# Five buffers for gathered rows and one residual tile, with the rows queued anew, in a streaming encoder step

## The chip, the cores and the metric

The kernel runs on one core of a Trainium2 chip. The time is device microseconds (us) of one execution. The engines are PE (TensorE), DVE (VectorE), ACT (ScalarE), POOL (GpSimd) and SP (SyncE), which here only issues transfers; POOL issues the gathers.

## The reference

One layer of a streaming encoder for 1024 prompt tokens and 32 sample tokens of width 1024, in f32:

```python
z = x @ w_in + b_in                       # split into 12 sections of 1024 columns
y_a = (a_b * conv3(a_c * a_x)) @ w_out_a                      # mixer A
y_b = (gelu(b_g) * rg_lru(conv4(b_x))) @ w_out_b              # mixer B
y_c = (rmsnorm(hgrn2(c_q, c_f, c_i)) * silu(c_g)) @ w_out_c   # mixer C, 8 heads
m = sigmoid(g_a)*y_a + sigmoid(g_b)*y_b + sigmoid(g_c)*y_c
x = layer_norm(ALPHA*x + m @ w_o)                             # x1 in the kernel
# peer: 8 heads, product keys, the best 16 of 16384 experts for each head and token
h = gelu(x . u[expert]);  out = sum_k g_k * h_k * v[expert_k] # 128 experts a token
x = layer_norm(ALPHA*x + out)
```

## The kernel before

The tokens go in two halves of 512 (the second with the 32 sample tokens). The first half runs through mixers, `norm1` (L878) and `topk` first. Its four tiles of 128 tokens then take the expert rows one by one: `gather` (L1206) issues for each of 128 places an indirect transfer on POOL that brings one row of 1024 floats for each of 128 tokens (a buffer `row` from `big`, L869), 128 times from table u and 128 times from v. DVE takes the dot of a u row with x1 (L1222), or adds a v row, scaled, to x1 (L1230). The tile `x1g` holds x1 and collects the sum; at the end of a tile `ln` (L861 to L867) normalises it, with two `row` buffers for its gain and bias (L874), and SP stores it. That makes 4 x 256 = 1024 row instructions on DVE.

The second half's experts are done densely: the one-hot tiles `oa` and `ob` (L1072, L1075) spread the chosen weights over all 16384 experts through PE, and `dense` (L1106 on, blocks D0 to D15) multiplies by all of u and v. A part of the hidden layer is computed ahead, beside the spread, and read back in D0 to D4 (`ge<-hd`).

PE's matmuls are made of three products of a high and a low part (L336, L337, L341). A weight comes as `wraw` by SP; ACT makes its high part `wh` (L295) and DVE its low part `wl` (L299), or `wl` is fetched again from DRAM. In `dense`, DVE and ACT make `w`, `dh` and `dl` (L1126 to L1131) from the hidden layer.

The row instructions run beside the second half. `BESIDE` says how many of them belong to each of seven stretches of the program: the end of the first half's topk with mixer A (92), the heads of mixer C (125), the outputs of mixers C and B (145), out_b1, norm1 and topk1 (94), retrieval and spread with the hidden layer ahead (42), D0 to D4 (82), D5 to D15 (444). `pacing` (L1248) puts row k of r of a stretch behind the DVE instruction that stands where k/r of the stretch's PE instructions have been written; `paced` holds a row instruction behind that place in DVE's order. It is an earliest place: a scheduler that plans with transfer times sets the final order of each queue at build time, and it plans with the number of buffers.

```python
x1 = self.gp.tile([128, D], F32, name="x1g", tag="x1g", bufs=X1G)
nc.sync.dma_start(x1[:n], self.x1d[g0:g0 + n, :])
```

Of the kernel before, what the change touches and what calls it, by code (L numbers as in the profile page):

```python
# [10 lines left out]
F32 = mybir.dt.float32  # L11
# [10 lines left out]
D = 1024  # L22
# [32 lines left out]
MARK = lambda nc, n: None  # L55


BESIDE = 92, 125, 145, 94, 42, 82, 444
AHEAD = 40
LATE = 4  # L60
ORDER = (0, 0), (0, 1), (0, 2), (0, 3), (1, 2), (1, 3), (1, 0), (1, 1)
# [8 lines left out]
PL2 = True  # L70
F2 = 1
FA = 2
X1G = 2
HEAD = 4
TAIL = 4

# [25 lines left out]
class K:  # L102
# [764 lines left out]
        V.tensor_add(dst[:n], r[:n], bias[:n])  # L867

    def big(self):  # L869
        return self.gp.tile([128, D], F32, name="row", tag="row", bufs=4)  # L870

    def lnvec(self, nm, pool=None, bufs=None):
        t = pool.tile([128, D], F32, name=nm, bufs=bufs) if pool else self.big()
# [332 lines left out]
    def gather(self, ti, g0, n, ex, gw):  # L1206
# [9 lines left out]

        x1 = self.gp.tile([128, D], F32, name="x1g", tag="x1g", bufs=X1G)
        nc.sync.dma_start(x1[:n], self.x1d[g0:g0 + n, :])
# [29 lines left out]
def pacing(ins, cuts, rows):  # L1248


    E, out = mybir.EngineType, []
    for i0, i1, r in zip(cuts, cuts[1:], rows):
        at, n, j = [], 0, 0
        for i in ins[i0:i1]:
            n += i.engine == E.PE
            if i.engine == E.DVE:
                at.append((n, i))
        n = int(n * (EARLY if i1 == cuts[-1] else 1.0))
        for k in range(r):
            while j + 1 < len(at) and at[j][0] < n * k // r:  # L1260
                j += 1
            out.append(at[j][1])
    return out


def build(tc, io):
    with ExitStack() as ctx:
# [64 lines left out]
        k.cuts.append(len(ins))  # L1332
        k.pace, k.npaced = pacing(ins, k.cuts, BESIDE), 0
        for t in todo:
# [63 lines left out]
```

## Time and profile before

| | us |
|---|---|
| median of 3 runs | 4093.62 |
| lowest and highest | 4083.32, 4103.83 |
| the profiled execution's own time | 4081.6 |
| its span in the profile | 4079.8 |

The span goes from the first to the last instruction of the profiled execution. Times in the views count from its start. Busy time of an engine is the sum of its instructions' durations; a wait is idle time of an engine and is put down to what ended it.

### The profile page before, as it was taken

The numbers are of one execution on the slowest core, as the hardware profiler recorded it, in microseconds if no ns is written. First come the engines' busy times: TensorE is split into PE (matmuls) and PEld (weight loads), VectorE is DVE, ScalarE is ACT, GpSimd is POOL, SyncE is SP. The second block draws the span as 40 slices with busy tenths as digits, with TensorE's granted clock in tenths as the row PEclk, the third lists the DMA queues.
The fourth block names the chain that finished last, engine by engine and source line by source line (L and its number), as shares of the span: only waits on it lengthen the run. The fifth ranks groups of instructions, "written<-read, shape, count | busy, mean of one in ns | idle before, by whom it ended". The sixth has DMA issues, their size and how long they took to land.

```text
span 4079.8 us, 69919 instructions
## 1 busy us (share of the span) xinstructions
PE 3794.9 (93%) x26917; PEld 3544.5 (87%) x26917; DVE 3139.8 (77%) x6578; ACT 1495.5 (37%) x2368; POOL 1537.8 (38%) x1353
## 2 busy tenths in 40 slices
PE   9999999999899898999778998799999999999996
PEld 7888787788899887999668998689999999999996
DVE  6556435579988887775679999788788888778888
ACT  3333327433232213563233588722222222222222
POOL 0000000001345544343333688723355555455553
PEclk9999999999999998999889999899999999999998
DMA  5443455678999887999997897798899988889996
GB/s 190 145 145 132 150 192 178 221 242 300 355 325 318 305 286 249 350 333 342 363 347 276 281 284 231 221 340 313 289 323 324 325 315 315 307 308 315 315 327 231
DMA packets 377230, 1132.94 MB, mean 278 GB/s; under 512 B 34816, under 2 KB 109696, under 8 KB 374848
## 3 DMA queue, kind: packets, MB, share of 16 engines
q1 hardware_dynamic: 229440, 591.53, 41.2%
q0 software_dynamic: 147456, 536.94, 37.5%
q8 instruction: 212, 3.47, 0.3%
q14 instruction: 122, 1.00, 0.1%
HBM read 1000.48 MB, written 127.84 MB: 277 GB/s over the span
## 4 chain that ended last, share of the span: by engine, by line
issue 12%; DVE 12%; DMA 10%; PE 9%; POOL 8%; ACT 1%; POOLq 0%; DVEq 0%; SPq 0%; ACTq 0%
POOL row L1213 8%; DMA row<-in_v,ex 8%; DVE x1g L1230 3%; PE z L341 3%; PE z L337 2%; PE z L336 2%; DVE oa L1072 2%; DMA row<-in_u,ex 2%; DVE wl L299 1%; PE t L1076 1%; DVE e L963 1%; DVE e L962 0%; DVE e L965 0%; DVE e L964 0%; DVE e L961 0%
## 5 line engine op out<-in xcount | busy, mean ns | idle before, releaser
L336 PE MATMUL z<-h,wh 128*128 128x272 f32 (+5 forms) x4608 | 1319.0, 313 | 43.0 <-ACT wh L295 25.5
L337 PE MATMUL z<-l,wh 128*128 128x272 f32 (+5 forms) x4608 | 1307.9, 311 | 1.2 <-DVE l L372 1.2
L1213 POOL DMA_INDIRECT row<-in_u,ex x512 | 621.2, 1213 | 1497.8 <-DVE ex L1036 651.6
L295 ACT CAST wh<-wraw 128x1024 fp32r<-128x1024 f32 x568 | 596.1, 1050 | 1419.2 <-PE z L337 1102.9
L336 PEld LDWEIGHTS z<-h,wh 128*128 128x128 f32 x4608 | 879.7, 191 | 89.1 <-ACT wh L295 28.7
L1213 POOL DMA_INDIRECT row<-in_v,ex x512 | 680.3, 1329 | 663.0 <-DVE x1g L1230 450.6
L337 PEld LDWEIGHTS z<-l,wh 128*128 128x128 f32 x4608 | 880.9, 191 | 37.6 <-issue 2.9
L341 PE MATMUL z<-h,wl 128*128 128x272 f32 (+5 forms) x4608 | 741.8, 309 | 7.5 <-DMA wl<-wl 6.6
L1230 DVE SCALAR_TENSOR_TENSOR x1g<-row,hh,x1g 128x1024 f32<-128x1024 f32 x512 | 654.9, 1279 | 119.5 <-DMA row<-in_v,ex 115.7
L1222 DVE SCALAR_TENSOR_TENSOR row<-row,x1g 128x1024 f32<-128x1024 f32 x512 | 619.3, 1219 | 152.6 <-DMA row<-in_u,ex 151.8
L341 PEld LDWEIGHTS z<-h,wl 128*128 128x128 f32 x4608 | 648.1, 189 | 42.4 <-DMA wl<-wl 8.0
L299 DVE TENSOR_TENSOR wl<-wraw,wh 128x1024 fp32r<-128x1024 f32 x400 | 488.4, 1222 | 188.4 <-ACT wh L295 88.1
L337 PE MATMUL z<-dl,wh 128*128 128x272 f32 x2048 | 521.0, 294 | 21.5 <-DVE dl L1131 21.1
L336 PE MATMUL z<-dh,wh 128*128 128x272 f32 x2048 | 516.4, 294 | 9.6 <-ACT dh L1130 8.9
L337 PEld LDWEIGHTS z<-dl,wh 128*128 128x128 f32 x2048 | 388.3, 194 | 27.7 <-DVE dl L1131 27.7
L336 PEld LDWEIGHTS z<-dh,wh 128*128 128x128 f32 x2048 | 386.3, 193 | 12.8 <-ACT dh L1130 12.1
L341 PE MATMUL z<-dh,wl 128*128 128x272 f32 x2048 | 284.6, 292 | 23.5 <-DVE wl L299 23.5
L341 PEld LDWEIGHTS z<-dh,wl 128*128 128x128 f32 x2048 | 270.5, 192 | 25.3 <-DVE wl L299 25.3
L1075 POOL TENSOR_SCALAR ob<-iota,tr 128x128 f32<-128x128 f32 x272 | 215.2, 805 | 34.8 <-ACT tr L1050 23.8
L1130 ACT CAST dh<-w 128x544 fp32r<-128x544 f32 x128 | 82.5, 648 | 374.4 <-DVE w L1126 360.6
L1076 PE MATMUL t<-ob,oa 128*128 128x128 f32 x1088 | 169.0, 294 | 30.8 <-DVE oa L1072 11.2
L1076 PEld LDWEIGHTS t<-ob,oa 128*128 128x128 f32 x1088 | 148.9, 201 | 44.3 <-POOL ob L1075 17.2
(379 smaller groups left out, 4600.4 us busy)
## 6 DMA issues: line engine op xcount, KB each, us to landing
wl<-wl SPq DMA_DIRECT2D x304, 512.0 KB
wraw<-in_w_in SPq DMA_DIRECT2D x192, 512.0 KB
wraw<-in_vt SPq DMA_DIRECT2D x128, 512.0 KB
wraw<-in_ut SPq DMA_DIRECT2D x128, 512.0 KB
gd<-stg SPq DMA_DIRECT2D x34, 1024.0 KB
gt<-gd SPq DMA_DIRECT2D x16, 2176.0 KB
wraw<-in_wq SPq DMA_DIRECT2D x56, 512.0 KB
wraw<-in_w_o SPq DMA_DIRECT2D x24, 512.0 KB
```

Of the source, the lines that this page charges most:

```text
L295: nc.scalar.copy(wh, raw)
L299: nc.vector.tensor_sub(wl, raw, wh.bitcast(F32))
L336: mm(ps[:, :n], wh[:, k, :], xh[:, o:o + n], start=k == 0, stop=False)
L337: mm(ps[:, :n], wh[:, k, :], xl[:, o:o + n], start=False, stop=False)
L341: mm(ps[:, :n], wl[:, k, :], xh[:, o:o + n], start=False, stop=k == KT - 1)
L1072: V.tensor_scalar(oa, self.iota, tr[:, 0, t:t + 1], tr[:, 2, t:t + 1], op0=OP.is_equal, op1=OP.mult)
L1075: G.tensor_scalar(ob, self.iota, tr[:, 1, t:t + 1], None, op0=OP.is_equal)
L1076: nc.tensor.matmul(pw[:, s * 128:(s + 1) * 128], oa, ob, start=True, stop=True)
L1130: A.copy(hi, w)
L1213: nc.gpsimd.indirect_dma_start(out=u[:n], out_offset=None, in_=self.io[tab], in_offset=bass.IndirectOffsetOnAxis(ap=ex[:n, s:s + 1], axis=0))
L1222: V.scalar_tensor_tensor(u[:n], u[:n], 1.0, x1[:n], op0=OP.mult, op1=OP.mult, accum_out=hh[:n, s:s + 1])
L1230: V.scalar_tensor_tensor(x1[:n], u[:n], hh[:n, s:s + 1], x1[:n], op0=OP.mult, op1=OP.add)
```

## The change

`row` gets five buffers in place of four, `x1g` one in place of two (SBUF for one buffer of 128 x 1024 floats goes from one to the other). The number of row instructions rises from 145 to 185 beside the outputs and from 94 to 135 in out_b1, norm1 and topk1; it falls from 42 to 30 beside retrieval and spread, from 82 to 40 in D0 to D4 and from 444 to 417 in D5 to D15. The first two numbers stay, and so does the sum of 1024.

```diff
-BESIDE = 92, 125, 145, 94, 42, 82, 444
+BESIDE = 92, 125, 185, 135, 30, 40, 417
@@
-X1G = 2
+X1G = 1
@@
     def big(self):
-        return self.gp.tile([128, D], F32, name="row", tag="row", bufs=4)
+        return self.gp.tile([128, D], F32, name="row", tag="row", bufs=5)
```

## Rows read from the trace of the kernel before

**Rows 1.** The first two parts of the page: busy time of each engine with its share of the span, and the mean DMA rate in 40 equal slices of 102 us.

```profile
PE 3794.9 (93%) x26917; PEld 3544.5 (87%) x26917; DVE 3139.8 (77%) x6578; ACT 1495.5 (37%) x2368; POOL 1537.8 (38%) x1353
...
GB/s 190 145 145 132 150 192 178 221 242 300 355 325 318 305 286 249 350 333 342 363 347 276 281 284 231 221 340 313 289 323 324 325 315 315 307 308 315 315 327 231
```

**Rows 2.** The chain of work that ended last, shares of the span by engine and line.

```profile
POOL row L1213 8%; DMA row<-in_v,ex 8%; DVE x1g L1230 3%; PE z L341 3%; PE z L337 2%; PE z L336 2%; DVE oa L1072 2%; DMA row<-in_u,ex 2%; DVE wl L299 1%; PE t L1076 1%; DVE e L963 1%; DVE e L962 0%; DVE e L965 0%; DVE e L964 0%; DVE e L961 0%
```

**Rows 3.** Busy time of each engine in four stretches between row instructions at which `BESIDE` goes on (first and last row of a stretch, in DVE's order): the outputs' 145 rows, the 94 after them, the 82 of D0 to D4, the 444 of D5 to D15. Columns: stretch, its length, busy time (instructions), granted clock as a share of full, busy share of the DMA engines, GB/s.

```profile
1579.00:2026.00 447.00, 415.07 (x3075) 404.84 (x3074) 299.49 (x517) 203.18 (x295) 175.09 (x146) 0.96 0.92 342
2026.00:2366.00 340.00, 289.14 (x2162) 279.79 (x2163) 311.43 (x1036) 137.11 (x263) 158.90 (x147) 0.91 0.87 304
...
2650.00:2937.00 287.00, 268.09 (x1997) 262.00 (x1996) 228.58 (x357) 69.40 (x85) 87.54 (x82) 0.95 0.89 316
2937.00:4050.00 1113.00, 1076.39 (x8458) 1071.03 (x8456) 924.90 (x1180) 296.10 (x445) 600.44 (x441) 0.99 0.89 315
```

**Rows 4.** The instructions on the tile `row`: lowest, median and highest duration in ns, first and last start.

```profile
L1222 DVE SCALAR_TENSOR_TENSOR row<-row,x1g x512: 1196/1218/1292, 976.3 to 3730.8; 128x1024 f32<-128x1024 f32 x171
...
L1213 POOL DMA_INDIRECT row<-in_v,ex x512: 932/1178/5040, 1331.7 to 4043.0; - x171
L1230 DVE SCALAR_TENSOR_TENSOR x1g<-row,hh,x1g x512: 1175/1279/1400, 1341.3 to 4049.7; 128x1024 f32<-128x1024 f32 x171
```

**Rows 5.** The chain in order of time, in the stretch of D5 to D15: start, duration, what.

```profile
3119.00 8.20 DMA row<-in_v,ex
3131.02 5.38 DMA row<-in_v,ex
```

**Rows 6.** Waits from 2937 to 4050 us: who waited for what, us in total, times, longest.

```profile
POOL row L1213 <- DVE x1g L1230: 241.7, 180, 7.4
POOL row L1213 <- DVE row L1222: 202.7, 132, 7.4
DVE x1g L1230 <- DMA row<-in_v,ex: 84.6, 67, 5.6
...
DVE row L1222 <- DMA row<-in_u,ex: 64.3, 41, 7.1
```

**Rows 7.** Two lines of the program with their first and last start: the gates beside mixer B (their last one ends the outputs), and the products with the keys (the last one ends topk1 on PE).

```profile
L836 ACT ACTIVATE e<-z,hb x48: 480/496/693, 357.9 to 1838.8; 128x274 f32<-128x274 f32 x32, 128x512 f32<-128x512 f32 x16
...
L938 PE MATMUL t<-keys,e x288: 270/275/583, 880.1 to 2213.9; 128*128 128x128 f32 x128, 128*32 128x128 f32 x16
```

**Rows 8.** Busy time as in rows 3, in three other stretches.

```profile
1579.00:2110.00 531.00, 468.23 (x3427) 453.67 (x3427) 356.84 (x630) 225.07 (x348) 209.88 (x174) 0.94 0.93 344
2110.00:2600.00 490.00, 441.22 (x3349) 425.49 (x3349) 487.80 (x1631) 312.40 (x597) 318.82 (x341) 0.95 0.82 264
980.00:1060.00 80.00, 63.78 (x478) 60.47 (x477) 76.53 (x299) 25.65 (x39) 26.64 (x26) 0.96 1.02 398
```

**Rows 9.** The same view for instructions on the tile `row` alone; the columns are DVE (its dots count twice, with the read of their sum), POOL (one per gather), clock, DMA share and GB/s.

```profile
1579.00:2110.00 531.00, 215.40 (x303) 209.88 (x174) 0.94 0.93 344
2110.00:2600.00 490.00, 127.68 (x100) 125.22 (x100) 0.95 0.82 264
2600.00:2650.00 50.00, 10.24 (x8) 8.88 (x8) 0.93 0.77 241
```

**Rows 10.** DVE's waits for rows: from 976 to 1248 us (one line), from 1248 to 1579 us (two), from 1579 to 2110 us (two).

```profile
DVE row L1222 <- DMA row<-in_u,ex: 13.5, 11, 2.3
...
DVE x1g L1230 <- DMA row<-in_v,ex: 15.1, 11, 3.2
DVE row L1222 <- DMA row<-in_u,ex: 14.1, 12, 3.0
...
DVE row L1222 <- DMA row<-in_u,ex: 57.1, 42, 4.4
...
DVE x1g L1230 <- DMA row<-in_v,ex: 14.2, 10, 4.1
```

**Rows 11.** DVE's costliest groups from 2110 to 2600 us: busy us, mean ns, and the idle time before them with what ended it.

```profile
L1072 DVE TENSOR_SCALAR oa<-iota,tr 128x128 f32<-128x128 f32 x487 | 153.0, 388 | 0.2
L1230 DVE SCALAR_TENSOR_TENSOR x1g<-row,hh,x1g 128x1024 f32<-128x1024 f32 x100 | 127.7, 1277 | 1.9 <-DMA row<-in_v,ex 1.9
```

**Rows 12.** The end of a tile on DVE, from the instructions on the tile `x1g`.

```profile
L861 DVE BATCH_NORM_STATS2 lnst<-x1g x8: 665/676/694, 1691.2 to 4054.5; 128x6 f32<-128x512 f32 x8
...
L865 DVE TENSOR_SCALAR x1g<-x1g,lnmv x4: 794/808/812, 1696.6 to 4058.8; 128x1024 f32<-128x1024 f32 x4
L866 DVE TENSOR_TENSOR x1g<-x1g,row x4: 1215/1216/1224, 1697.5 to 4059.7; 128x1024 f32<-128x1024 f32 x4
```

**Rows 13.** Two transfers of 512 KB on the chain that ended last.

```profile
2069.02 12.73 DMA x1n<-in_x
...
4045.45 5.36 DMA row<-in_ln_b
```

**Rows 14.** PE on that chain: 16 matmuls of 128x272.

```profile
2671.09 2.00 PE z L341 x16
```

**Rows 15.** PE's waits from 2650 to 2937 us (one line) and from 2937 to 4050 us (three).

```profile
PE z L337 <- DVE dl L1131: 15.6, 12, 2.7
...
PE z L341 <- DVE wl L299: 23.5, 8, 5.6
PE z L336 <- ACT dh L1130: 6.1, 4, 2.8
PE z L337 <- DVE dl L1131: 5.5, 6, 2.0
```

## The prediction

> **What bounds the kernel now.** I read the busy totals first: PE is busy for 93% of the span, DVE for 77%, and POOL, which issues the gathers and builds one-hot tiles, for 38% [rows 1]. So PE is the engine to feed, and the question is what starves it. The chain that ended last does not run through PE alone: the gathers, as POOL's issue (8%) and as transfers (8% and 2%), hold some 18% of the span [rows 2]. The reader is to see there that the chain of gathered rows (buffer free, POOL issues, the row lands, DVE accumulates, buffer free) competes with PE for the end.
>
> Then the windows, cut where the list `BESIDE` hands over, that is at row 217, 362, 498 and 580 in the order of accumulation [rows 3]. Each row is 0.524 MB and its DVE instruction takes 1.22 us for u and 1.28 us for v [rows 4]. In the last stretch (D5 to D15) 444 rows in 1113 us are one each 2.51 us; with four buffers a buffer comes round each 10.0 us. That is what it needs: transfers on the chain there take 5.4 to 8.2 us, and issue (0.9 to 1.2 us) and accumulation are added [rows 4, 5]. POOL waits 445 us of this stretch for DVE to free a buffer, and DVE 149 us for rows to land [rows 6]: four buffers are just too few. DVE works in order, so behind a late row stands the split of the next weights (wl) and of the activations (dh, dl) for PE.
>
> The same holds earlier, by another sign. The last output gate beside mixer B is done at 1839 us [rows 7], but the 145 rows queued beside the outputs last until 2026 us, 190 us into the next stage [rows 3]. From 1579 to 2110 us there are 174 gathers, one each 3.05 us [rows 9]; the list asks for more than comes. So here it is not the list that sets the pace but the four buffers, and DVE still waits 71 us for rows in that stretch, 29 us in the heads, 13 us before [rows 10].
>
> Last, the stretch in which DVE is full: from 2110 to 2600 us (topk1, retrieval, spread) it is busy for 488 of 490 us [rows 8] and waits 1.9 us for rows; 100 rows take 128 us of it, beside 153 us of one-hot tiles [rows 11]. An added row there costs its full 1.28 us.
>
> **The change, part by part.**
>
> *Heads and before (976 to 1579 us), list unchanged.* The fifth buffer gives a row 25% more time. DVE's 42 us of row waits [rows 10] are the most that it can give back. The heads are a chain of short DVE and PE steps, so a DVE wait is often PE's too, but the weights are ahead of it; between all and nothing I take half: **-20** (0 to -42).
>
> *Outputs to norm1 (1579 to 2110 us), list 145 to 185 and part of 94 to 135.* If the buffers set the pace, five give 174 x 1.25 = 217 rows, 43 more. DVE has room: 357 busy of 531 us [rows 8], 55 more fit. DMA: 344 GB/s x 531 us = 183 MB, and 22.5 MB more make 205 MB, 386 GB/s. The 80 us from 980 us show 398 GB/s [rows 8], so it just fits; at the best of the 102 us slices, 363 GB/s [rows 1], it takes 565 us, +34. The 71 us of row waits can shrink, or stay if denser traffic makes rows later; half of them at most would be PE's. I take **-5** (-35 to +34), near the row of 398, because that one is as mixed with weights as this stretch.
>
> The Trainium skill, "DMA: Bandwidth & Descriptors", section "Where 436 GB/s comes from", says that a transfer between HBM and SBUF is bound by about 358 GB/s a core; by that figure the stretch would take 573 us, an estimate, and 42 us of gain would go. This trace does not agree over 80 us (398 GB/s [rows 8]) and nearly does over each 102 us slice (363 at most [rows 1]).
>
> *DVE-full stretch and the end of the spread (2110 to 2650 us).* Now it does 108 rows (100 and 8) [rows 9]. The new list has 92+125+185+135+30 = 567 rows up to the dense stage; with 217 + 217 = 434 done at 2110 us, 133 are left, 25 more: 25 x 1.28 = 32 us. The end of the second tile also moves here (row 512 is number 110 of the 135; before it was in D0 to D4): two statistics, one normalisation, two passes, 0.68 x 2 + 0.81 + 1.22 x 2 = 4.6 us [rows 12]. Sum **+37**. Bounds: if the fifth buffer speeds up nothing, 217 + 174 = 391 are done and 176 left, 68 more: +92. If rows kept to the list, which spreads 135 over the matmuls from 1839 us to the end of topk1 at 2214 us [rows 7], 98 of these and 217 + 185 = 402 before them were done and 67 left: -48. I take the middle, what five buffers give.
>
> *D0 to D4 (2650 to 2937 us), list 82 to 40.* PE does 1997 matmuls [rows 3]; at full rate 16 take 2.00 us [rows 14], so the floor is 250 us of the 287. What PE waits for there is dl, from DVE [rows 15]. 42 rows fewer take 54 us from DVE (229 busy) and 22 of 91 MB from DMA [rows 3]. I take two thirds of the 37: **-24** (-10 to -37).
>
> *D5 to D15 (2937 us on), list 444 to 417.* Floor 8458 x 0.125 = 1057 us of 1113. Rows come each 2.67 us; five buffers give each 13.3 us against the 10 it needs, so most of DVE's 149 us of row waits [rows 6] go, with 35 us of its work. PE's visible waits are 35 us, 24 of them for wl [rows 15], the rest of the 56 sits between. I take a little over half, **-30** (-10 to -50).
>
> *One residual tile instead of two.* Now the next tile's first dots run between the last passes of the one before. With one tile: last pass, store of y, load of x1, first dot. In SP's queue the weights stand behind that load, and in DVE's the splits for PE behind the first dot. A load of the same size took 12.7 us on the chain in heavy traffic, one at the end 5.4 us [rows 13]: a store and a load make 11 to 25 us a turn, three turns. DVE has other work in that time, and the next tile's rows are already being gathered; what it costs is what the queue order misjudges. Nothing in the trace shows that; I take **+8** (0 to +36, half of three long turns), nearer to nothing, since PE has weights in hand.
>
> Sum: -20 - 5 + 37 - 24 - 30 + 8 = **-34 us**. The profiled execution took 4081.6 us, 12 under the median of 4093.62; taken from the median, 4060 us.
>
> **Rivals.** About 0.5% (20 us) is what a measurement of this kernel can tell from no change: the three runs before lie within 20.5 us.
>
> *The chain of rows is the bound (larger gain).* 18% of the chain goes through rows [rows 2]. If so, the waits go nearly whole: -42 - 35 in front, -37 - 50 behind, against +37 + 8: about -119, 3975 us. For it: POOL's waits for buffers. Against: PE runs at 95% of full rate in D5 to D15 already.
>
> *DMA at its limit (no change).* If 363 GB/s is all that lasts, the outputs and norm1 cost +34 instead of -5: sum +5, 4099 us. For it: DMA moves 344 GB/s there at 0.93 of its engines. Against: the 398, at 1.02 [rows 8].
>
> *Rows pile up in the DVE-full stretch (slower).* The list asks for 567 rows before the dense stage whether or not they come in time, and what is late is done where DVE has no room. Break-even: the other terms make -20 - 5 - 24 - 30 + 8 = -71, so the stretch loses it all at +71, which is (71 - 5)/1.28 = 52 rows more, that is if only 407 are done at 2110 us: if the fifth buffer speeds the rows from 1579 us up by under 9%. With no speed-up (+92) and less to win behind (-10 - 15), the sum is -20 + 0 + 92 - 25 + 8 = +55, 4149 us. For it: rows here may be late because of DVE's queue and loaded DMA rather than the number of buffers. Against: in the last stretch four buffers' turn and a row's time are equal.
>
> **Chances.** Forecast (20 to 80 us gained) 0.48, larger gain 0.12, no change 0.22, slower 0.18. Faster 0.60, same 0.22, slower 0.18. The forecast's own range is 4014 to 4074. The range for 8 in 10 reaches halfway into the larger gain and into the slower case: 4005 to 4112 us.
>
> **What would show it.** DVE's waits for rows in D5 to D15 fall from 149 us to under 50; that stretch is some 30 us shorter, D0 to D4 24 us. From 1579 us to the end of norm1 the gathers come each 2.4 to 2.6 us at 380 GB/s or more. The spread ends later, measured from the end of norm1, by some 37 us. At the turns of a tile there are 11 to 25 us without a row. I am wrong if the rows between 1579 and 2110 us are no denser (then slower), if PE loses time there to late weights (DMA), or if the last stretch is no shorter although DVE no longer waits for rows: then PE was not waiting for DVE.

## The result, and the profile after

The change makes the kernel slower: 4119.42 us against 4087.81 us (medians of 7 runs each), a ratio of 1.0076 with a 95% interval of 1.0058 to 1.0095, some 32 us. The forecast was 34 us faster, the range ended at 4112. The profiled execution took 4113.9 us, with a span of 4112.1 us.

The page's busy line and its chain, for the changed kernel:

```profile
PE 3806.3 (93%) x26917; PEld 3552.8 (86%) x26917; DVE 3140.1 (76%) x6578; ACT 1507.7 (37%) x2367; POOL 1536.2 (37%) x1353
...
PE z L341 12%; PE z L336 12%; PE z L337 12%; PE t L1076 2%; DMA row<-in_u,ex 1%; DVE oa L1072 1%; DVE x1g L1230 1%; DVE row L1222 1%; DMA ge<-hd 1%; DMA row<-in_v,ex 1%; POOL row L1213 1%; DMA wl<-wl 1%; DVE e L963 0%; DVE e L962 0%; DVE e L965 0%
```

The rows have left the chain: 3% of the span, against 18% in [rows 2]. PE's matmuls hold it now. By this view alone the change did what it should; it is no view of the time.

The stretches between the places where the list goes on, as in [rows 3]: the 185 rows of the outputs, the 135 after them, the 40 of D0 to D4, the 417 of D5 to D15.

```profile
1569.00:2073.00 504.00, 454.91 (x3263) 435.10 (x3264) 360.76 (x602) 209.40 (x309) 226.00 (x187) 0.94 0.95 358
2073.00:2604.00 531.00, 446.39 (x3325) 433.12 (x3323) 504.86 (x1587) 289.37 (x551) 329.18 (x327) 0.90 0.86 287
...
2730.00:3012.00 282.00, 265.88 (x2017) 260.44 (x2017) 174.79 (x277) 67.44 (x85) 38.36 (x41) 0.97 0.70 241
3012.00:4060.00 1048.00, 1042.26 (x8295) 1041.28 (x8294) 883.76 (x1108) 302.65 (x442) 549.92 (x412) 1.00 0.90 321
```

The last row shows the gain: PE is busy for 1042 of 1048 us where it was for 1076 of 1113. DVE's waits from 3012 to 4060 us, to be set beside [rows 6], where rows made it wait 149 us:

```profile
DVE acc L1144 <- PE z L341: 75.5, 54, 4.8
DVE wl L299 <- ACT wh L295: 53.8, 43, 4.3
DVE row L1222 <- DMA row<-in_u,ex: 12.5, 8, 5.3
...
DVE x1g L1230 <- DMA row<-in_v,ex: 0.7, 3, 0.3
```

DVE now waits for PE, and 13 us for rows. Where the time went is seen when the traces are cut at events of the program instead of rows. The table is worked out from the traces: the ends are the last start of a line's instruction (attention L767 for the heads, L846 in out_b1, L906 for norm1, the keys' products L938 for topk1, the one-hot products L1076 for the spread), then the first `w` of D0, the first of D5 and the last matmul. Rows are the row instructions on DVE up to or in a stretch. The kernels from e1 on are those of the experiments. Each line is one traced execution, which lies up to 14 us from its kernel's median; e4_x1g's is the fastest of its ten.

| kernel | to heads' end | outputs, out_b1 | norm1 | topk1 | spread | to D0 | D0 to D4 | D5 to D15 | after PE | rows done by end of topk1 | rows in spread |
|---|---|---|---|---|---|---|---|---|---|---|---|
| before | 1571 | 380 | 140 | 123 | 417 | 23 | 287 | 1108 | 31 | 421 | 75 |
| after | 1561 | 398 | 143 | 129 | 489 | 18 | 285 | 1064 | 25 | 456 | 110 |
| e1_bufs | 1564 | 400 | 147 | 125 | 379 | 24 | 287 | 1064 | 30 | 452 | 45 |
| e2_list | 1575 | 385 | 142 | 121 | 440 | 30 | 312 | 1065 | 25 | 427 | 88 |
| e4_x1g | 1568 | 380 | 140 | 121 | 423 | 24 | 286 | 1105 | 32 | 418 | 78 |
| e7_more | 1563 | 395 | 147 | 129 | 497 | 27 | 295 | 1056 | 25 | 456 | 119 |
| e8_split | 1568 | 399 | 141 | 125 | 446 | 31 | 295 | 1065 | 25 | 452 | 88 |
| e5_late | 1563 | 396 | 147 | 115 | 362 | 18 | 300 | 1068 | 45 | 440 | 22 |
| e9_thin | 1568 | 382 | 101 | 114 | 431 | 28 | 336 | 1059 | 30 | 365 | 85 |
| e10_back | 1559 | 398 | 125 | 103 | 360 | 19 | 286 | 1086 | 125 | 405 | 22 |
| e11_none | 1560 | 399 | 140 | 126 | 379 | 24 | 271 | 1059 | 169 | 452 | 45 |
| e12_halfdve | 1554 | 393 | 146 | 127 | 416 | 19 | 282 | 1058 | 25 | 470 | 96 |
| e13_halfdma | 1598 | 381 | 134 | 111 | 467 | 18 | 280 | 1061 | 25 | 470 | 96 |

After against before: -10 to the end of the heads, +18 in outputs and out_b1, +3 and +6 in norm1 and topk1, **+72 in the spread**, -5, -2 in D0 to D4, **-44 in D5 to D15**, -6 at the end: +32.

Busy time in the spread of the changed kernel (2231 to 2720 us), for all instructions:

```profile
2231.00:2720.00 489.00, 393.58 (x2833) 376.26 (x2832) 454.39 (x1327) 318.72 (x613) 365.15 (x383) 0.87 0.82 259
```

and for those on `row` alone (DVE, POOL, clock, DMA share, GB/s):

```profile
2231.00:2720.00 489.00, 140.10 (x166) 143.21 (x111) 0.87 0.82 259
```

The same for the kernel before (2214 to 2631 us), all instructions, then those on `row`:

```profile
2214.00:2631.00 417.00, 372.04 (x2829) 357.39 (x2828) 413.08 (x1231) 309.98 (x609) 313.59 (x346) 0.96 0.80 251
```

```profile
2214.00:2631.00 417.00, 96.21 (x76) 98.34 (x74) 0.96 0.80 251
```

Take rows from DVE's busy time: 454 - 140 = 314 us and 413 - 96 = 317 us. The other work is the same; rows are +44 us and DVE's idle time +31 us (35 against 4). DVE's longest wait there in total, after:

```profile
DVE row L1222 <- DMA row<-in_u,ex: 24.8, 10, 6.2
```

25 us of the idle time are rows again. All ten of these waits stand behind the turn from the second tile to the third, between 2564 and 2699 us; the new list brings that turn here, and the single residual tile makes it long. Instructions on `x1g` from 2480 to 2540 us, with count, duration in ns (lowest, median, highest), first and last start:

```profile
L1230 DVE SCALAR_TENSOR_TENSOR x1g<-row,hh,x1g x2: 1271/1328/1385, 2480.1 to 2484.8; 128x1024 f32<-128x1024 f32 x2
...
L867 DVE TENSOR_TENSOR x1g<-x1g,row x1: 1216/1216/1216, 2516.1 to 2516.1; 128x1024 f32<-128x1024 f32 x1
L1232 SPq DMA_DIRECT2D out_y<-x1g x1: 338/338/338, 2517.3 to 2517.3; - x1
L1218 SPq DMA_DIRECT2D x1g<-x1d x1: 319/319/319, 2522.2 to 2522.2; - x1
...
L1222 DVE SCALAR_TENSOR_TENSOR row<-row,x1g x4: 1208/1210/1214, 2534.2 to 2539.3; 128x1024 f32<-128x1024 f32 x4
```

From the last v row (2484.8) to the first dot (2534.2) there are 49 us without a row: 31 until the last pass, which stands among the one-hot tiles, 5 for the store, 12 for the load. DVE idles only 1 us in them, it has other work. But 54 of the stretch's 110 rows are left for the 186 us behind the turn, and there they stand ahead of the spread's own work. One of PE's waits for that work, from 2480 to 2740 us after (first line) and from 2490 to 2650 us before (second):

```profile
PE t L1049 <- DVE e L1030: 24.8, 2, 17.7
...
PE t L1049 <- DVE e L1030: 7.3, 2, 4.8
```

The granted clock of the spread is 0.87 of full after and 0.96 before; PE waits more, and nearly the same matmuls keep it busy for 22 us longer. What that clock costs by itself no run here tells.

### The profile page after: what moved, and what is told of

Read it like the earlier page. It is cut to its first block, busy times and chain, and to the rows that moved or that the text cites. A ratio compares the mean times of both kernels' runs of the same rounds, so it can differ in the third digit from the quotient of the medians.

```text
span 4112.1 us, 69894 instructions
## 1 busy us (share of the span) xinstructions
PE 3806.3 (93%) x26917; PEld 3552.8 (86%) x26917; DVE 3140.1 (76%) x6578; ACT 1507.7 (37%) x2367; POOL 1536.2 (37%) x1353
## 4 chain that ended last, share of the span: by engine, by line
PE 37%; DVE 7%; DMA 4%; issue 1%; ACT 1%; POOL 1%; ACTq 0%; DVEq 0%; SPq 0%; POOLq 0%
PE z L341 12%; PE z L336 12%; PE z L337 12%; PE t L1076 2%; DMA row<-in_u,ex 1%; DVE oa L1072 1%; DVE x1g L1230 1%; DVE row L1222 1%; DMA ge<-hd 1%; DMA row<-in_v,ex 1%; POOL row L1213 1%; DMA wl<-wl 1%; DVE e L963 0%; DVE e L962 0%; DVE e L965 0%
## 5 line engine op out<-in xcount | busy, mean ns | idle before, releaser
L1230 DVE SCALAR_TENSOR_TENSOR x1g<-row,hh,x1g 128x1024 f32<-128x1024 f32 x512 | 654.3, 1278 | 33.6 <-DMA row<-in_v,ex 29.0
L1076 PE MATMUL t<-ob,oa 128*128 128x128 f32 x1088 | 187.9, 318 | 52.6 <-DVE oa L1072 25.0
L1076 PEld LDWEIGHTS t<-ob,oa 128*128 128x128 f32 x1088 | 165.4, 221 | 68.5 <-POOL ob L1075 34.7
L1144 DVE TENSOR_TENSOR acc<-acc,z 128x272 f32<-128x272 f32 x240 | 99.6, 432 | 140.4 <-PE z L341 139.0
```

The source lines that it names most:

```text
L1076: nc.tensor.matmul(pw[:, s * 128:(s + 1) * 128], oa, ob, start=True, stop=True)
L1144: V.tensor_add(v(acc[d]), v(acc[d]), p)
L1230: V.scalar_tensor_tensor(x1[:n], u[:n], hh[:n, s:s + 1], x1[:n], op0=OP.mult, op1=OP.add)
```

## The experiments

Two theories at first. List: the loss is the 81 rows that the new list adds before the spread (12 fewer are listed beside it, so 69 before the dense stage), done where DVE is full. Residual: the loss is the turn of a tile with one residual tile. Ratios are to the kernel before on the same chip; edits are shown against the changed kernel.

**Buffers and residual tile, old list (e1_bufs).**

```diff
-BESIDE = 92, 125, 185, 135, 30, 40, 417
+BESIDE = 92, 125, 145, 94, 42, 82, 444
```

> Five row buffers and one residual tile with the old list (92, 125, 145, 94, 42, 82, 444). List theory (the loss is the 81 rows listed before the dense stage; they are done where DVE is full): 30 to 60 us faster than before; topk1 to the end of the spread takes 420 to 445 us as before (431), and D5 to D15 loses nearly all of DVE's 149 us of row waits. Residual theory (the loss is the turn of a tile with one residual tile, 28 and 49 us without a row): within 15 us of before or slower, since all three turns stay.

4021.01 us, ratio 0.9832 (0.9793 to 0.9871): 65 us faster, as the list theory has it and a little more. The spread is not as before but 379 us: 452 rows are done by the end of topk1 where four buffers do 421, so only 45 of the 498 are left. In D5 to D15 PE is as little disturbed with 444 rows as after the change with 417, though DVE waits 41 us for rows there. This kernel beats both.

**List alone (e2_list).**

```diff
-X1G = 1
+X1G = 2
-        return self.gp.tile([128, D], F32, name="row", tag="row", bufs=5)
+        return self.gp.tile([128, D], F32, name="row", tag="row", bufs=4)
```

> The new list alone, with four row buffers and two residual tiles. List theory: at least as slow as the changed kernel, 30 to 80 us slower than before: topk1 to the end of the spread takes 500 us or more, and D5 to D15 keeps more than 80 us of row waits. Residual theory: within 15 us of before or faster, since no turn stops the rows.

4092.47 us, ratio 1.0013 (0.9996 to 1.0031): no change that can be told, as the residual theory had it. The list theory misses here: the spread takes 440 us, not 500. With four buffers DVE's queue order leaves 45 of the 567 rows for the dense stage (522 are done at its first `w`), and D0 to D4 pays for them (312 us). And D5 to D15 falls to 1065 us though DVE still waits 71 us for rows in it:

```profile
DVE row L1222 <- DMA row<-in_u,ex: 37.4, 42, 5.3
DVE x1g L1230 <- DMA row<-in_v,ex: 33.9, 40, 2.2
```

So 27 rows fewer or a fifth buffer do the same there, each alone; they do not add.

**Residual tile alone (e4_x1g).**

```diff
-BESIDE = 92, 125, 185, 135, 30, 40, 417
+BESIDE = 92, 125, 145, 94, 42, 82, 444
-        return self.gp.tile([128, D], F32, name="row", tag="row", bufs=5)
+        return self.gp.tile([128, D], F32, name="row", tag="row", bufs=4)
```

> One residual tile alone, four row buffers, old list. List theory: within 20 us of before (a turn stops the rows for some 25 us, but DVE has other work). Residual theory: 20 to 60 us slower than before, from three turns.

4094.5 us, ratio 1.0023 (1.0009 to 1.0037): 9 us slower. The residual theory falls, for the tile alone. The three turns last 23, 30 and 21 us from row to row (9, 8 and 10 before), and DVE has other work. So neither the list nor the tile costs much by itself with four buffers; the list costs where it is added to five buffers and one tile.

**Thirty rows more beside the spread (e7_more).**

```diff
-BESIDE = 92, 125, 185, 135, 30, 40, 417
+BESIDE = 92, 125, 185, 135, 60, 40, 387
```

> The changed kernel with 30 more rows beside retrieval and spread, taken from D5 to D15 (92, 125, 185, 135, 60, 40, 387). List theory: 30 x 1.28 = 38 us more in the spread and nothing back, since PE already runs without gaps in D5 to D15 of the changed kernel: 60 to 80 us slower than before. Residual theory: as the changed kernel, some 30 us slower than before.

4137.56 us, ratio 1.0128 (1.0089 to 1.0166): 52 us slower than before, 18 slower than the changed kernel. The sign is the list theory's, the size half: only 9 of the 30 land in the spread (119 rows, 497 us), 9 more come between its end and D0, and 12 spill into D0 to D4 (295 us).

**Same 567 rows, otherwise split (e8_split).**

```diff
-BESIDE = 92, 125, 185, 135, 30, 40, 417
+BESIDE = 92, 125, 145, 94, 111, 40, 417
```

> Five buffers, one residual tile, 567 rows listed before the dense stage as in the changed kernel, but 145, 94 and 111 of them beside outputs, norm1 with topk1, and retrieval with spread, in place of 185, 135 and 30. Residue theory (before the spread the buffers set how many rows get done, some 450 to the end of topk1; only the sum listed before the dense stage matters, since what is left is done in the spread): as the changed kernel, within 15 us, 25 to 40 us slower than before; 110 rows in the spread, which takes 480 to 495 us. Pile theory (a late list puts its rows ahead of the spread's own work, an even one costs 1.28 us a row): 25 us or more faster than the changed kernel, spread 455 to 465 us.

4096.39 us, ratio 1.0015 (1.0002 to 1.0028): 23 us faster than the changed kernel, between the two. By the end of topk1 452 rows are done of 456 listed, where the changed kernel does 456 of 537: the 81 rows that the new list adds there bring 4, and the others are overdue when the spread begins. An even pace puts 88 rows in the spread, not 110, and DVE idles 19 us there, not 35; 20 rows go over into the dense stage (D0 to D4 takes 295 us). So the sum of the list is the larger part (75 us against e1_bufs), and rows that are overdue the other (23 us).

**Fewer rows before the dense stage (e5_late).**

```diff
-BESIDE = 92, 125, 185, 135, 30, 40, 417
+BESIDE = 92, 125, 155, 70, 20, 100, 462
```

> Five buffers, one residual tile, few rows before the dense stage: 92, 125, 155, 70, 20, 100, 462 (462 in place of 567). Residue theory: some 10 rows are left for the spread, which takes 330 to 345 us (379 with 45 rows, at 1.27 us a row); D0 to D4 stays near 287 us with 100 rows, D5 to D15 takes 1064 to 1085 us with 462: 60 to 100 us faster than before. Rival (rows cost their DVE time wherever they are put): 52 rows x 1.28 us come back in the dense stage, no faster than the kernel with five buffers and the old list, 55 to 70 us faster than before.

4021.33 us, ratio 0.9836 (0.9813 to 0.9859): as fast as with the old list, where either reading would put it; the sum tells nothing. The residue theory's spread is missed: 22 rows are left for it, not some 10, and it takes 362 us, not 330 to 345. The parts tell more: the spread wins 17 us with 23 rows fewer (0.74 us each), D0 to D4 loses 13 with 18 more, and 14 rows are left after the last matmul.

**Few rows beside outputs and norm1 (e9_thin).** With five buffers, outputs to norm1 take 540 to 547 us against 520.

```diff
-BESIDE = 92, 125, 185, 135, 30, 40, 417
+BESIDE = 92, 125, 90, 60, 131, 82, 444
```

> Five buffers, one residual tile, the old list but with 90 and 60 rows beside outputs and norm1 with topk1, and 131 beside the spread (92, 125, 90, 60, 131, 82, 444; 498 before the dense stage as in the old list). Traffic theory (five buffers make the rows denser from the end of the heads to norm1, and their transfers delay PE's weights): that stretch falls from 547 us to 520 to 530, as with four buffers, while the spread gets the rows back and takes 40 to 60 us more. Rival (the stretch is longer because of one residual tile or of the order of DVE's queue): it stays at 540 us or more.

4048.95 us, ratio 0.9902 (0.9879 to 0.9926). The stretch falls to 483 us, further than expected, so the rival falls; norm1 alone falls from 147 to 101 us with 14 rows in it in place of 57. Here norm1 of this kernel:

```profile
1950.00:2051.00 101.00, 84.56 (x636) 79.67 (x635) 55.37 (x110) 39.69 (x82) 18.92 (x15) 0.97 0.92 337
```

and of the changed one:

```profile
1959.00:2102.00 143.00, 98.33 (x620) 89.50 (x619) 109.08 (x169) 43.02 (x85) 68.20 (x56) 0.80 1.00 394
```

PE does nearly the same matmuls; in the changed kernel the transfers run at 394 GB/s at a full share of the DMA engines, and the granted clock is 0.80 of full (part of the stretch at 1.2 GHz in place of 2.4), falling mostly at or just behind waits of PE of 2 to 8 us. The edit takes away the rows' time on DVE as well as their transfers, so it doesn't tell which of the two it was. The rows are paid for later, as expected: spread 431 us, and D0 to D4 336 us.

**Rows into the back (e10_back).**

```diff
-BESIDE = 92, 125, 185, 135, 30, 40, 417
+BESIDE = 92, 125, 150, 40, 20, 90, 507
```

> Five buffers, one residual tile, rows kept out of norm1, topk1 and the spread: 92, 125, 150, 40, 20, 90, 507. If rows cost most where the transfers or DVE are full and little in D5 to D15: norm1 takes 105 to 120 us (140 to 147 before), the spread 335 to 360, D0 to D4 290, D5 to D15 with 507 rows to the end 1120 to 1140 us (1094 with 444): 75 to 105 us faster than before, the fastest of all. Rival (with five buffers a row costs about 1 us wherever it is put, because each stretch is now full): within 15 us of the kernel with five buffers and the old list, 50 to 75 us faster than before.

4072.75 us, ratio 0.9966 (0.9955 to 0.9978). Missed by both. Before D5 it went nearly as hoped (norm1 125 us, spread 360; D5 begins at 2850 us, 2926 with the old list), but the back doesn't hold 507 rows: it takes 1211 us to the end, not 1120 to 1140. The stretch to the last matmul, and what follows it, for instructions on `row`:

```profile
2850.00:3936.00 1086.00, 558.45 (x709) 607.67 (x450) 0.99 0.91 326
3936.00:4061.00 125.00, 80.41 (x63) 81.85 (x57) 0.52 0.81 276
```

61 rows run after PE is done, one each 2 us. The gathers go at one each 2.41 us in D5 to D15 (1086/450); e11_none, with 526 listed, has the same pace (438 in 1059 us).

**No row in D0 to D4 (e11_none).**

```diff
-BESIDE = 92, 125, 185, 135, 30, 40, 417
+BESIDE = 92, 125, 145, 94, 42, 0, 526
```

> Five buffers, one residual tile, no rows beside D0 to D4: 92, 125, 145, 94, 42, 0, 526. If D0 to D4 is held by the serial start of each block (w, dh, dl before the first matmul) and not by rows, it stays at 280 us or more with no row in it (287 with 82 rows, 285 with 40). If rows hold it, it falls to 250 to 265 us, near PE's floor of 250. D5 to D15 with 526 rows: 1120 us or more to the last matmul (1064 with 444), if DVE has no room for 82 more rows.

One execution, 4129.41 us, since 87 rows are left after PE; D5 to D15 takes 1059 us to the last matmul, not 1120. D0 to D4 takes 271 us, between the two: 82 rows cost it 16 us, and 21 us over PE's floor have nothing to do with rows. PE's waits there of about 1 us stand at the start of the blocks, one every 52 us, before matmuls on dl. The sums of PE's two kinds of wait in D0 to D4 (2628 to 2899 us):

```profile
PE z L337 <- DVE dl L1131: 6.5, 10, 1.1
PE z L336 <- ACT dh L1130: 6.3, 14, 0.7
```

**Half the work on DVE (e12_halfdve), or half the transfer (e13_halfdma).** In the first DVE works on 512 of a row's 1024 columns; in the second 512 columns are gathered and used twice. The edits are shown in part: the first changes the v rows (L1230) in the same way, and the second makes two DVE instructions of each row.

```diff
-    V.scalar_tensor_tensor(u[:n], u[:n], 1.0, x1[:n], ...
+    V.scalar_tensor_tensor(u[:n, :512], u[:n, :512], 1.0, x1[:n, :512], ...
```

> The changed kernel with DVE working on 512 of the 1024 columns of each gathered row (the other half of the experts' sums is left out), transfers in full. If DVE's time is what a row costs in the spread, 110 rows x 0.6 us go: 489 us falls to 420 or less. If the traffic of the rows is what lengthens norm1, it stays at 135 us or more (143); if DVE's time does, it falls to 120 or less (101 us were seen with 14 rows in it).

```diff
-    nc.gpsimd.indirect_dma_start(out=u[:n], out_offset=None, in_=self.io[tab], ...
+    half = self.io[tab].rearrange("e (t d) -> (e t) d", t=2)
+    nc.gpsimd.indirect_dma_start(out=u[:n, :512], out_offset=None, in_=half, ...
```

> The changed kernel with half rows gathered (512 columns, from other places of the tables) and DVE working twice on them, so that its time stays about 1.3 us a row; the experts' sums are left out in this form. If traffic lengthens norm1, it falls from 143 us to 120 or less and PE's waits for wl there go; the spread stays at 470 us or more, since DVE's time is the same. If DVE's time lengthens norm1, it stays at 135 us or more.

One execution each, 4020.87 and 4077.79 us. With half of DVE's work the spread takes 416 us, with half the transfers 467 us (both with 96 rows), just under the 470 expected: in the spread a row's price is in the main DVE's time. Late transfers are a smaller part, since DVE's waits for rows fall from 25 to 9 us with half of them. In outputs and out_b1 the pair points to the transfers: 398 us in the changed kernel, 393 with half of DVE's work, 381 with half the transfers (380 before). For out_b1 alone (last gate matmul of mixer B to the last of out_b1) it is 138, 134 and 112 us. Here out_b1 of the changed kernel, then with half the transfers:

```profile
1821.00:1959.00 138.00, 123.57 (x911) 119.84 (x909) 87.17 (x154) 41.26 (x59) 58.24 (x51) 0.96 0.95 360
```

```profile
1867.00:1979.00 112.00, 111.20 (x871) 110.89 (x871) 93.76 (x268) 41.36 (x60) 56.80 (x54) 1.00 0.90 323
```

So it is in the main not DVE's time; that it is the transfers is likely, but not shown. The second stretch holds 40 matmuls fewer (5 us at full rate), and its kernel ends the heads 37 us later. With the rows thinned (e9_thin) out_b1 has nearly the same traffic, 329 GB/s, and takes 129 us. In norm1 neither half frees PE (146 and 134 us, with 57 and 56 rows), which fits neither theory; taking both away by taking the rows out did. In the second kernel a row costs DVE 1.5 us, so its norm1 is not quite a test of traffic alone.

## Why the prediction was wrong

**The chain of rows and D5 to D15: right, larger.** Forecast -30, measured -44 (and -6 behind PE). DVE's row waits fell from 149 to 13 us. But the reason given, fifth buffer and 27 rows fewer together, was one too many: with 444 rows the five buffers give the same 1064 us, and with four buffers 417 rows give 1065. Either has the whole gain alone; with the buffer in place the list's part was counted twice.

**D0 to D4: this step failed.** Forecast -24, measured -2. PE's waits for dl in [rows 15] were put down to rows in DVE's queue, and two thirds of the 37 us over PE's floor to 42 rows. The waits for dl are 16 us before, 11 after, 7 without any row; the last stand at the start of each block. 42 rows fewer do next to nothing to the stretch, 82 fewer give 16 us, and 21 of the 37 us are there without rows. Rows that are overdue where D0 begins cost it more: 336 us with 122 rows in e9_thin.

**DVE-full stretch: right mechanism, mis-sized.** Forecast +37, within a bound of +92; topk1 and spread measured +78. From 2110 us to the dense stage 42 rows more were done where 25 were reckoned, 35 of them in the spread, since by 2110 us 417 rows were done, not 434. The turn in the outputs, 29 us without rows in place of 9, took some seven of these (20 us at 2.7 us a row, an estimate); for the others the fifth buffer gave less than a quarter more. The spread's 35 are +44 us of DVE's time with the end of the tile. What the sum left out is the +31 us of idle DVE: an added row was to cost its 1.28 us and no more, but behind the turn DVE waited 25 us for overdue rows to land. The slower rival had named place and mechanism; its condition (five buffers speed the rows up by under 9%) was not met, they did by 13% (196 gathers for 174). The loss came at 42 rows more, not 52, because D0 to D4 gave nothing, the next step gave less than nothing, and a row cost more than its time on DVE.

**Outputs to norm1: this step failed in its sign.** Forecast -5, measured +21 from the end of the heads to the end of norm1. The stretch from 1579 to 2110 us of the changed kernel, to be set beside [rows 8]:

```profile
1579.00:2110.00 531.00, 463.15 (x3307) 442.73 (x3307) 381.93 (x639) 217.38 (x337) 242.36 (x196) 0.93 0.95 361
```

The gathers come one each 2.7 us at 361 GB/s, not 2.4 to 2.6 at 380 or more. In norm1 the transfers reach 394 GB/s, so the rival with its limit of 363 was wrong on the limit. What failed is that denser rows were costed at nothing where DVE and the transfers still had room. The runs show that they cost: outputs and out_b1 take 393 to 400 us in the kernels that gather whole rows into five buffers, 380 to 385 with four, and 382 with five and thinned rows, where norm1 falls too. DVE's time is not the reason (393 us with half of it); the transfers are the likely one. That they cost by making weights late for PE is not shown: PE's waits for wl, after from 1842 to 2110 us (first line), are much as they were before from 1842 to 2100 us (second).

```profile
PE z L341 <- DMA wl<-wl: 25.8, 7, 7.8
...
PE z L341 <- DMA wl<-wl: 23.2, 5, 8.5
```

The Trainium skill, "DMA: Bandwidth & Descriptors", section "Issuing engines are not separate DMA queues", says that transfers of all issuing engines run on the same 16 DMA engines and interleave. The trace agrees: in norm1 of the changed kernel the rows issued by POOL take 53% of these engines' time and the transfers issued by SP 47%.

**Heads: half.** Forecast -20, measured -10.

**One residual tile: right alone, open in the change.** Forecast +8, which no row bore out, as it says; alone, with four buffers, +9. In the changed kernel the turns last 29, 49 and 23 us, not 11 to 25. No run has five buffers and two residual tiles, so how much of the 31 us of idle DVE is the single tile's and how much the overdue list's stays open.

In one line: the fifth buffer with the single tile is worth -65 us, and the list takes back about 98 (4119 against 4021). The forecast let the list earn 24 us in D0 to D4 that were not there, and a share of the 30 behind that the buffer had earned already.

## What to carry to other kernels

When two edits relieve the same wait, cost each with the other in place: the second may find nothing left to win and keep only its price. A list that paces work in front of an engine is an earliest place; look at how many instructions are done by the end of each stage, because what is overdue falls into the next stage, and here that was the one where the engine was full. Before moving work into a stage, give it a price there even where no engine is full: from 1579 to 2110 us DVE was busy for 382 of 531 us and the DMA engines for 0.95 of their time, and the denser rows cost 21 us all the same.

## What was not expected of the hardware

HBM and SBUF exchanged 394 GB/s over the 143 us of norm1 in the changed kernel. The Trainium skill, "DMA: Bandwidth & Descriptors", section "Where 436 GB/s comes from", has about 358 GB/s a core as the bound for such transfers, half of a stack's 716; with one core running, the measurement differs.
